# Stick-breaking attention summed by parts, with differences of v's rows

## The chip, the cores and the metric

The kernel runs on one core of one Trainium2 chip. The time is that of one execution on the device in microseconds (us), from the start to the end of the program on that core. The time given for a kernel is the median of several runs. The profile comes from one more execution, taken by the hardware profiler. PE is TensorE (PEld its weight loads), DVE is VectorE, ACT is ScalarE, POOL is GpSimd, and SP is the engine whose queue issues most of the DMAs.

## The reference, cut to what matters

The program is a trunk of two layers over 1024 tokens of 1024 channels; each layer is followed by a mixture of experts. The change touches one part of layer 0, stick-breaking attention with 8 heads of 64 channels:

```python
for blk in range(seq // Q_BLOCK):                      # Q_BLOCK = 128
    z = jnp.einsum('bhqd,bhkd->bhqk', qb, kb) * scale  # keys up to the block's end
    causal = kpos < qpos
    log_1m = jnp.where(causal, jax.nn.log_sigmoid(-z), 0.0)
    between = lax.cumsum(log_1m, axis=3, reverse=True) - log_1m
    wts = jnp.where(causal, jnp.exp(jax.nn.log_sigmoid(z) + between), 0.0)
    outs.append(jnp.einsum('bhqk,bhkd->bhqd', wts, vb))
```

So the weight of key k for a query is sigmoid(z_k) times the product of sigmoid(-z_j) over all later keys j. Everything is float32.

With pr_k the product of sigmoid(-z_j) from key k to the last key of the block, and pr = 1 behind the last key, the weight of key k is pr_(k+1) - pr_k, since sigmoid(z) = 1 - sigmoid(-z). A sum of (pr_(k+1) - pr_k) v_k over k equals v of the last key of the block plus the sum of pr_k (v_(k-1) - v_k), where v before the first key is 0.

## The kernel before

**Layer 0 ahead of attention.** The input projection gives the convolution's gate and value, q, k and v. Products are made in three matmuls of split operands (`mm3`, L260 to L264: high times high, high times low, low times high). The depthwise convolution of 31 taps runs on DVE (L482, 31 instructions of 1024 columns for each of 4 channel tiles) beside PE's projections. v is projected last (`vproj`, L528): for each of 8 tiles of 128 tokens, 24 matmuls whose stationary operand is the normalized input `hh`, `hl` and whose moving operand is v's weights give a PSUM tile `pvt` of 128 tokens by 512 channels; ACT copies it to `vsb` (L537). The calls of `vproj` stand between the steps of other work: three tiles behind the sums of squares of q and k (`qks`, L548, copied by DVE in L550), one each ahead of the stages of the convolution's layer norm (L576 to L596, sums over channels by matmuls on PE, L348), and two behind the last Silu (L600). Here the order of the instructions on each engine is set by a scheduler when the program is built, from priorities and its own costs; on the chip each engine takes its queue in order.

**The attention loop.** From L614 on, the order on ACT, DVE, PE and POOL is the order of the program. There are 4 pairs of heads (c), 8 query tiles each (t), taken in the order 3, 2, 1, 0, 4, 5, 6, 7; a tile's keys are taken from the last in blocks of up to 512 (bi counts them), so that there are 48 steps. A step works on 128 queries of two heads and n keys, n being 128 to 512. In loop turn s the program issues:

- `scores(s+1)`: matmuls of q and k to `z` (L653), and on the diagonal block the mask (L657);
- `mod_close`: two transposes on PE (`pmc`, L289) and a reduce on DVE (L290), which end a piece of an unrelated product, the layers' modulation vectors;
- `breaks(s)`: on ACT the sigmoid of -z (s1, L669) and of z (s2, L671) for both heads; on DVE the edge column of `pr` (1 at the start, L673, or the carry, L675), the running product of s1 from the last key to the first (two scans, L678), and the weights `w` = s2 times pr one column on (L681);
- `turn(s-1)`: n/128 transposes for each head to PSUM (`pt`, L690) and ACT's copy of them to `wt` (L692);
- `values(s-2)`: matmuls of `vsb` and `wt` to `po` (L703); at the end of a group of four query tiles ACT copies `po` to `o` (L708);
- `mod_open`, in most turns: 16 matmuls of the next modulation piece (`pm`, L277), DVE's copy of the sums to `modev` (L280), and the issue on SP of the loads of a later piece;
- in 24 turns, a part of the next pair's q or k: copies on ACT (L631, L632) and a subtraction on POOL (L634).

`pm` and `pmc` share one PSUM buffer, `pt` and `po` have one each, and `z` has four.

**After it** comes the output projection (from L774), whose order is again that of the program; its weights are loaded during the loop. It begins with ACT's and DVE's split of the weights (L252, L253).

## Time and profile before

| | |
|---|---|
| median of 3 runs | 2169.33 us (2169.12 to 2172.84) |
| the profiled execution | 2171.37 us, span 2169.6 us |
| busy over the span | PE 1863.1 us (86%), DVE 1429.3 (66%), ACT 989.7 (46%), POOL 424.9 (20%) |
| v's projection and the layer norm | about 229 to 318 us of the span |
| attention loop, first scores to last values | about 326 to 554 us |
| mean granted TensorE clock, in parts of the full one | 0.935 |

A page of the profile gives busy times of each engine and its instructions by line. Busy time of PE is modelled at its end, since matmuls overlap. A line such as `L280 DVE COPY modev<-pm 128x256 f32 x39 | 16.4, 420 | 10.2 <-PE pm L277 10.1` means: 39 instructions, 16.4 us busy, 420 ns each; the engine stood idle for 10.2 us just ahead of them, and PE's instruction of line 277 ended 10.1 us of that. In a timeline a line begins with start and length in us.

### The profile page before, as it was taken

What the parts mean: (1) busy time and instruction counts of PE and PEld (TensorE: products, weight loads), DVE (VectorE), ACT (ScalarE), POOL (GpSimd) and SP (SyncE); (2) the same over time, 40 slices, a digit from 0 to 9 for tenths busy, and PEclk for the clock granted to TensorE, in tenths of its full rate; (3) what the DMA queues carried; (4) which work ended last, traced back from release to release, by engine and by line L of the source; (5) the groups of instructions that cost most, each with busy time, mean ns of one, the idle gap of its engine ahead of it and who ended that gap; (6) DMA issues with size and microseconds to landing.
All of it is one profiled execution on the core that took longest, in us unless ns stands there. A gap on an engine that the chain in (4) does not pass through costs nothing. (4 is left out here: it accounts for less than half of the span.)

```text
span 2169.6 us, 27608 instructions
## 1 busy us (share of the span) xinstructions
PE 1863.1 (86%) x9580; PEld 1435.8 (66%) x9580; DVE 1429.3 (66%) x2110; ACT 989.7 (46%) x1388; POOL 424.9 (20%) x264
## 2 busy tenths in 40 slices
PE   6999987888886899988797599999868989888884
PEld 3788565555775677767676478887747777666663
DVE  4699657887588755676655266566784553677781
ACT  3212236776422544454544257784124342465660
POOL 1312004330233101110111132212331110211110
PEclk9999998999997899999999799999879999999997
DMA  8111004566522876897967521105325763899991
GB/s 304 58 39 59 20 20 137 194 208 220 176 107 92 279 232 208 238 321 226 291 190 245 148 92 44 44 20 186 117 103 183 201 198 114 259 299 296 309 308 28
DMA packets 104514, 369.52 MB, mean 170 GB/s; under 512 B 13680, under 2 KB 15024, under 8 KB 104240
## 3 DMA queue, kind: packets, MB, share of 16 engines
q1 hardware_dynamic: 91216, 319.29, 42.8%
q0 software_dynamic: 12928, 46.67, 9.6%
q8 instruction: 157, 2.57, 0.5%
q14 instruction: 117, 0.96, 0.1%
q10 hardware_dynamic: 96, 0.03, 0.0%
HBM read 324.76 MB, written 41.19 MB: 169 GB/s over the span
## 5 line engine op out<-in xcount | busy, mean ns | idle before, releaser
L253 DVE TENSOR_TENSOR wt<-raw,wt 128x1024 fp32r<-128x1024 f32 x384 | 459.1, 1222 | 144.7 <-ACT wt L252 116.2
L252 ACT ACTIVATE wt<-raw 128x1024 fp32r<-128x1024 f32 x384 | 395.5, 1059 | 213.0 <-DMA raw<-in_ex_w_dram 165.8
L262 PE MATMUL h<-wt,xtF 128*128 128x512 f32 x512 | 217.2, 424 | 15.1 <-PEq L1423 5.2
L263 PE MATMUL h<-wt,xtF 128*128 128x512 f32 x512 | 209.1, 408 | 6.7 <-issue 6.7
L264 PE MATMUL h<-wt,xtF 128*128 128x512 f32 x512 | 209.4, 409 | 4.3 <-issue 3.7
L482 DVE SCALAR_TENSOR_TENSOR cacc<-u,vecs,cacc 128x1024 f32<-128x1024 f32 x116 | 149.5, 1289 | 3.5
L262 PE MATMUL yp<-wt,xtF 128*128 128x512 f32 x256 | 109.5, 428 | 29.4 <-ACT xtF L1231 25.2
L253 POOL TENSOR_TENSOR wl<-raw,wh 128x1024 fp32r<-128x1024 f32 x32 | 84.4, 2658 | 243.8 <-ACT wh L252 243.8
L262 PEld LDWEIGHTS h<-wt,xtF 128*128 128x128 f32 x512 | 101.4, 198 | 44.1 <-issue 18.2
L264 PEld LDWEIGHTS h<-wt,xtF 128*128 128x128 f32 x512 | 101.0, 197 | 31.9 <-issue 5.9
L263 PEld LDWEIGHTS h<-wt,xtF 128*128 128x128 f32 x512 | 101.8, 199 | 29.0 <-issue 9.0
L262 PE MATMUL pout<-wouth,ch 128*128 128x512 f32 x256 | 110.3, 431 | 3.3 <-ACT ch L252 1.7
L264 PE MATMUL yp<-wt,xtF 128*128 128x512 f32 x256 | 107.6, 420 | 6.4 <-DVE xtF L1232 6.2
L1212 ACT ACTIVATE xtF<-pxt 128x512 fp32r<-128x512 f32 x64 | 34.9, 594 | 162.0 <-PE pxt L1211 146.6
L263 PE MATMUL pout<-woutl,ch 128*128 128x512 f32 x256 | 103.9, 406 | 2.8 <-DVE woutl L253 2.8
L263 PE MATMUL yp<-wt,xtF 128*128 128x512 f32 x256 | 106.2, 415 | 0.0
L264 PE MATMUL pout<-wouth,cl 128*128 128x512 f32 x256 | 104.1, 407 | 0.1
L262 PEld LDWEIGHTS yp<-wt,xtF 128*128 128x128 f32 x256 | 51.8, 203 | 50.3 <-ACT xtF L1231 30.9
L277 PE MATMUL pm<-raw,condb 128*32 128x256 f32 x768 | 63.1, 451 | 19.0 <-DMA raw<-in_mod_w_dram 13.5
L1200 POOL DMA_INDIRECT out_dram<-y,sidx x16 | 30.7, 1918 | 237.0 <-DVE y L1240 196.0
L1213 DVE TENSOR_TENSOR xtF<-pxt,xtF 128x512 fp32r<-128x512 f32 x64 | 41.2, 685 | 53.4 <-ACT xtF L1212 53.3
L1500 POOL DMA_INDIRECT xg<-h2d,idx x45 | 53.6, 1190 | 83.6 <-PE h L262 30.8
(400 smaller groups left out, 4304.0 us busy)
## 6 DMA issues: line engine op xcount, KB each, us to landing
raw<-in_ex_w_dram SPq DMA_DIRECT2D x384, 512.0 KB, 6.0
raw<-in_mod_w_dram SPq DMA_DIRECT2D x96, 512.0 KB, 4.6
raw<-in_ev_w_dram SPq DMA_DIRECT2D x16, 512.0 KB, 4.4
raw<-in_od_in_dram SPq DMA_DIRECT2D x16, 512.0 KB, 4.3
h2d<-x SPq DMA_DIRECT2D x14, 512.0 KB, 2.6
xs<-in_x_dram SPq DMA_DIRECT2D x8, 512.0 KB, 7.8
raw<-in_ev_out_dram SPq DMA_DIRECT2D x8, 512.0 KB, 4.9
x<-in_x_dram SPq DMA_DIRECT2D x8, 512.0 KB, 4.4
```

Source lines behind the costliest of these rows:

```text
L252: nc.scalar.activation(hi, raw, AF.Copy)
L253: (lo_eng or nc.vector).tensor_tensor(lo, raw, hi.bitcast(F32), op=ALU.subtract)
L262: nc.tensor.matmul(out, ah, bh, start=start, stop=False)
L263: nc.tensor.matmul(out, ah, bl, start=False, stop=False)
L264: nc.tensor.matmul(out, al, bh, start=False, stop=stop)
L277: nc.tensor.matmul(pm[32 * g:32 * g + 32, 0:256], self.condb[:, k, :], raw[k // 4][:, g, :], start=k < 4, stop=k >= 4)
L482: nc.vector.scalar_tensor_tensor(y if j < CW - 1 else acc[:, c, :], u[:, j:j + S], self.vec("ev_dw_w", 4 * j + c), y, op0=ALU.mult, op1=AL ...
L1200: nc.gpsimd.indirect_dma_start(out=xacc, out_offset=bass.IndirectOffsetOnAxis(ap=col, axis=0), in_=y[0:n], in_offset=None, compute_op=ALU.add)
L1212: nc.scalar.activation(xt[:, q, 0], px, AF.Copy)
L1213: nc.vector.tensor_tensor(xt[:, q, 1], px, xt[:, q, 0].bitcast(F32), op=ALU.subtract)
L1500: self.nc.gpsimd.indirect_dma_start(out=dst, out_offset=None, in_=self.h2d[l], in_offset=bass.IndirectOffsetOnAxis(ap=col, axis=0))
```

## The change

v is now projected with channels on partitions: for each of 4 channel tiles and both halves of the tokens, 24 matmuls with the weights as the stationary operand give 128 channels by 512 tokens. ACT copies the column of the last token of each of the four 128-token tiles to `vlast` and the whole tile to one half of a buffer `vdiff` (it takes the place of one of the convolution's two input buffers). DVE subtracts each token's column from the one before it. One unit later PE turns the result into rows by four transposes, and ACT copies these into `vsb`. In the attention loop `pr` itself is turned and multiplied with `vsb`; the sigmoid of z, the edge column and the product w go, and `pr` has three buffers. When a group of four query tiles is done, ACT writes `o` in four pieces of 128 columns, each with the matching column of `vlast` added.

```diff
-        def vproj(ts):
-            pv = [psA.tile([P, HS], F32, name="pvt", tag="big") for _ in ts]
...
-            for t in ts:
-                nc.scalar.activation(vsb[:, t, :], pv[t - ts[0]], AF.Copy)
+        diffs, both = {}, up.tile([P, CW - 1 + S], F32, name="vdiff", tag="u")
+        def vproj(us):
+            for u in us:
+                c, hf = divmod(u, 2)
+                pv = psA.tile([P, HS], F32, name="pvt", tag="big")
+                sl, n = slice(HS * hf, HS * hf + HS), slice(P * c, P * c + P)
+                for q, (wh, wl) in enumerate(vw):
                     for k in range(4):
-                        self.mm3(pv[t - ts[0]], hh[:, 4 * q + k, sl], hl[:, 4 * q + k, sl], wh[:, k, :], wl[:, k, :],
+                        self.mm3(pv, wh[:, k, n], wl[:, k, n], hh[:, 4 * q + k, sl], hl[:, 4 * q + k, sl],
                                  q == 0 and k == 0, q == 1 and k == 3)
+                d = diffs[u] = both[:, HS * (u % 2):HS * (u % 2) + HS]
+                nc.scalar.activation(vlast[:, c, 4 * hf:4 * hf + 4], pv[:, P - 1::P], AF.Copy)
+                nc.scalar.activation(d, pv, AF.Copy)
+                nc.vector.tensor_tensor(d[:, 1:HS], pv[:, 0:HS - 1], d[:, 1:HS], op=ALU.subtract)
+                if hf:
+                    nc.vector.tensor_tensor(d[:, 0:1], vlast[:, c, 3:4], d[:, 0:1], op=ALU.subtract)
+                else:
+                    nc.vector.tensor_scalar(d[:, 0:1], d[:, 0:1], -1.0, None, op0=ALU.mult)
+                if u:
+                    vrows(u - 1)
+        def vrows(u):
+            c, hf = divmod(u, 2)
+            d, pt = diffs.pop(u), psA.tile([P, 4, P], F32, name="pvr", tag="big")
+            for j in range(4):
+                nc.tensor.transpose(pt[:, j, :], d[:, P * j:P * j + P], self.ident)
+            nc.scalar.activation(vsb[:, 4 * hf:4 * hf + 4, P * c:P * c + P], pt, AF.Copy)
...
         vproj((6, 7))
+        vrows(7)
         p1.close()
...
-            pr = w3.tile([P, 2, HS + 1], F32, name="pr", tag="pr")
-            w = ws_[s] = w3.tile([P, 2, HS], F32, name="w", tag="w")
+            pr = ws_[s] = w3.tile([P, 2, HS], F32, name="pr", tag="pr", bufs=3)
...
-            for hd in range(2):
-                nc.scalar.activation(s2[:, hd, 0:n], z[hd][:, 0:n], AF.Sigmoid, scale=rq[:, t, c, 0, hd:hd + 1])
-            if bi == 0:
-                nc.vector.memset(pr[:, :, n:n + 1], 1.0)
-            else:
-                nc.vector.tensor_copy(pr[:, :, n:n + 1], carry[0][:, :, 0:1])
...
-            nc.vector.tensor_tensor(w[:, :, 0:n], s2[:, :, 0:n], pr[:, :, 1:n + 1], op=ALU.mult)
...
-                nc.scalar.activation(o[:, c, sl], po[0], AF.Copy)
+                for j in range(4):
+                    u = t // 4 * 4 + j
+                    nc.scalar.activation(o[:, c, P * u:P * u + P], po[0][:, P * j:P * j + P], AF.Identity,
+                                         bias=vlast[:, c, u:u + 1])
```

## Rows read from the trace of the kernel before

**Rows 1.** The first line of the page.

```profile
span 2169.6 us, 27608 instructions
```

**Rows 2.** Busy time of each engine (count of instructions) in three stretches, with the granted TensorE clock, the DMA engines' busy share and GB/s.

```profile
229.00:318.00 89.00, 88.82 (x468) 54.30 (x466) 52.60 (x86) 24.69 (x38) 4.71 (x2) 1.00 0.04 12
318.00:326.00 8.00, 2.49 (x30) 1.22 (x34) 4.33 (x6) 7.56 (x13) 2.52 (x2) 0.77 0.44 131
326.00:554.00 228.00, 188.57 (x1810) 127.69 (x1804) 178.39 (x280) 160.16 (x291) 70.14 (x44) 0.92 0.56 188
```

The columns are PE, PEld, DVE, ACT and POOL, after the stretch and its length.

**Rows 3.** PE's groups by line from 326 to 554 us: busy time, mean ns, and the idle time of PE ahead of them with what ended it.

```profile
L653 PE MATMUL z<-ks,qs 128*128 128x512 f32 (+3 forms) x192 | 53.5, 403 | 1.8 <-ACT s L671 0.9 <-POOL ks L634 0.5 <-DVE ks L634 0.4
...
L690 PE MATMUL pt<-ident,w 128*128 128x128 f32 x288 | 43.7, 293 | 11.8 <-DVE pr L673 7.9 <-DVE pr L675 2.2 <-DVE w L681 1.7
...
L289 PE MATMUL pmc<-ident,modev 128*128 128x128 f32 x78 | 17.4, 307 | 23.1 <-DVE modev L280 22.9
...
L304 PE MATMUL pmt<-ident,mcol 128*32 128x128 f32 x2 | 0.5, 269 | 2.6 <-DVE mcol L320 2.6
```

**Rows 4.** The timeline of one full step (512 keys), PE and DVE.

```profile
386.08 0.44 PE L289 MATMUL pmc<-ident,modev 128*128 128x128 f32 x2 [1.32 <-DVE modev L280]
...
386.56 0.17 DVE L290 TENSOR_REDUCE mcol<-pmc 128x2 f32<-128x8 f32 x1 [0.53 <-PE pmc L289]
...
386.71 2.45 DVE L678 TENSOR_TENSOR_SCAN pr<-s,pr 128x512 f32<-128x512 f32 x2
...
389.26 1.23 DVE L681 TENSOR_TENSOR w<-s,pr 128x1024 f32<-128x1024 f32 x1
...
390.40 0.42 DVE L280 COPY modev<-pm 128x256 f32<-128x256 f32 x1
...
390.88 0.44 PE L289 MATMUL pmc<-ident,modev 128*128 128x128 f32 x2 [0.44 <-DVE modev L280]
```

**Rows 5.** PE's timeline around a short step (256 keys and fewer).

```profile
456.60 0.43 PE L289 MATMUL pmc<-ident,modev 128*128 128x128 f32 x2
...
460.27 0.43 PE L289 MATMUL pmc<-ident,modev 128*128 128x128 f32 x2
```

**Rows 6.** Groups by line from 326 to 554 us on DVE, ACT and POOL.

```profile
L681 DVE TENSOR_TENSOR w<-s,pr 128x1024 f32<-128x1024 f32 (+3 forms) x48 | 51.9, 1081 | 5.2
L671 ACT ACTIVATE s<-z,rqk 128x512 f32<-128x512 f32 (+3 forms) x96 | 50.6, 588 | 0.0
...
L634 POOL TENSOR_TENSOR ks<-qk,ks 64x512 fp32r<-64x512 f32 x28 | 48.0, 1714 | 40.6 <-ACT ks L632 36.8 <-issue 2.8
...
L692 ACT ACTIVATE wt<-pt 128x1024 f32<-128x1024 f32 (+3 forms) x48 | 39.1, 814 | 53.9 <-PE pt L690 53.7
...
L634 POOL TENSOR_TENSOR qs<-qk,qs 64x512 fp32r<-64x512 f32 x14 | 19.2, 1370 | 61.6 <-ACT qs L632 61.4
...
L708 ACT ACTIVATE o<-po 128x512 f32<-128x512 f32 x7 | 4.2, 602 | 0.2 <-PE po L703 0.2
```

**Rows 7.** PE's timeline in the loop: of the six waits ahead of pt the first and the last, and of the ten waits of over 1.14 us ahead of pmc the first and the last.

```profile
337.79 1.97 PE L690 MATMUL pt<-ident,w 128*128 128x128 f32 x8 [4.67 <-DVE pr L673]
...
360.14 0.69 PE L289 MATMUL pmc<-ident,modev 128*128 128x128 f32 x2 [2.12 <-DVE modev L280]
...
523.35 0.44 PE L289 MATMUL pmc<-ident,modev 128*128 128x128 f32 x2 [1.65 <-DVE modev L280]
...
551.41 1.06 PE L690 MATMUL pt<-ident,w 128*128 128x128 f32 x8 [1.70 <-DVE w L681]
```

**Rows 8.** ACT's groups by line and shape from 326 to 554 us: a sigmoid of 128 columns from PSUM.

```profile
L669 ACT ACTIVATE s<-z,nrq 128x128 f32<-128x128 f32 x16 | 4.9, 357 | 0.0
```

**Rows 9.** PE's timeline in the output projection: four transposes between matmuls of 512 columns.

```profile
571.89 0.60 PE L847 MATMUL pto<-ident,x 128*128 128x128 f32 x4
...
572.56 0.40 PE L263 MATMUL pout<-woutl,ch 128*128 128x512 f32 x1
```

**Rows 10.** Groups by line from 229 to 318 us.

```profile
L585 DVE TENSOR_TENSOR acc<-acc,rb_ps 128x512 f32<-128x512 f32 x8 | 4.9, 683 | 0.8 <-PE rb_ps L360 0.8
...
L537 ACT ACTIVATE vsb<-pvt 128x512 f32<-128x512 f32 x7 | 4.1, 593 | 22.5 <-PE pvt L264 22.5
...
L550 DVE COPY qkssev<-qks 128x512 f32<-128x512 f32 x2 | 1.4, 692 | 15.7 <-PE qks L548 15.7
```

**Rows 11.** Timelines of DVE (first line, the convolution's last tap) and PE (the others) in that stretch and at its end.

```profile
274.78 1.27 DVE L482 SCALAR_TENSOR_TENSOR acc<-u,vecs,cacc 128x1024 f32<-128x1024 f32 x1
...
287.57 1.06 PE L348 MATMUL ss<-acc,ones 128*32 128x512 f32 x8
...
317.25 0.39 PE L263 MATMUL pvt<-wl,hh 128*128 128x512 f32 x1
317.48 0.40 PE L264 MATMUL pvt<-wh,hl 128*128 128x512 f32 x1
319.42 1.07 PE L277 MATMUL pm<-raw,condb 128*32 128x256 f32 x16 [1.54 <-issue]
```

**Rows 12.** The timeline of POOL and DVE around one of POOL's pairs of products.

```profile
378.95 4.33 POOL L634 TENSOR_TENSOR ks<-qk,ks 64x512 fp32r<-64x512 f32 x2 [4.58 <-ACT ks L632]
...
380.94 1.26 DVE L678 TENSOR_TENSOR_SCAN pr<-s 128x512 f32<-128x512 f32 x1
...
382.12 2.24 DVE L678 TENSOR_TENSOR_SCAN pr<-s 128x512 f32<-128x512 f32 x1
```

## The prediction

> **What bounds the kernel now.** The head of the page comes first [rows 1]: the profiled execution has a span of 2169.6 us and took 2171.37, so 1.8 lie around the span; the median of the runs shown, 2169.33, is 2.0 below that execution. The table by stretches is next [rows 2]. Two stretches matter. From 229 to 318 us, where v is projected, PE is busy 88.82 of 89 us: there whatever PE does in addition is paid. From 326 to 554 us is the attention loop, 228 us for 48 steps, and no engine fills it: PE 188.6, DVE 178.4, ACT 160.2. So in that stage something goes in a circle. PE's groups by line, with the idle time ahead of each and what ended it, name it [rows 3]: of the 39.4 us that PE stands idle (228 less 188.6), 23.1 come ahead of the two transposes called pmc, which close a piece of the modulation product and need DVE's copy modev, and 11.8 ahead of pt, the turn of the weights w, which need DVE's product; 2.6 and 1.8 come ahead of pmt and z. The timeline of one full step shows the circle [rows 4]: pmc on PE at 386.08, DVE's small reduce at 386.56, two scans until 389.16, the product w at 389.26, the copy modev at 390.40, and the next pmc at 390.88, after PE stood idle for 0.44. The round is 4.80 us, and all of it is DVE in its queue order plus the hop to PE and back. PE's own work in it is 4.80 - 0.44 = 4.36 us. In a short step [rows 5] pmc follows pmc after 3.67 us with no idle time noted on PE: there PE already sets the pace.

> **The change part by part.** In the attention loop three things go: 96 second sigmoids, 50.6 us of ACT; 48 products w, 51.9 us of DVE [rows 6]; and DVE's small fill of the edge column in each step. ACT's share is worth nothing by itself: ACT waits for PE's pt in the stage, and the sigmoids that remain are ahead of the scans in its queue. DVE's share lies on the circle. From the start of w to the start of the copy behind it are 1.14 us [rows 4], so DVE's round falls from 4.80 to 3.66 and PE's 4.36 is late next: a full step gains its idle 0.44 and no more. The stage therefore cannot give more than PE's 39.4 us, and I work out what stays. Of the waits ahead of pmc, those below 1.14 go altogether; the ten above it, the first and last of which are in [rows 7] and which sum to 16.6, keep 16.6 - 10 x 1.14 = 5.2. The waits ahead of pt are six, 4.67 the first and 1.70 the last [rows 7], with 1.79, 1.78, 1.45 and 0.42 between; each loses the product's 1.23 [rows 4] and together they keep 5.2. The 2.6 ahead of pmt stays, since its chain is not touched. Of the 1.8 ahead of z half waits for the second sigmoid and goes, 0.9 stays. That leaves 13.9 and gives 39.4 - 13.9 = 25.5 us. Bounds: nothing at the one end, the full 39.4 at the other; I take 25.5 because the rounds are told one by one. [...]

> The output of each group of four query tiles is now written by four ACT instructions of 128 columns with a bias, not one of 512: 8 x 4 = 32 of them. The nearest row is a sigmoid of 128 columns, 0.357 [rows 8], against 0.60 for the one that goes [rows 6]: 8 x (4 x 0.357 - 0.60) = 6.6 us more on ACT. Behind them in ACT's queue stand the next step's sigmoids, for which the scans wait; ACT has just lost 50.6 us, so I put 1.5 of the 6.6 on the path (0 to 6.6).

> In the projection the 192 matmuls stay, with the roles of weights and moving operand exchanged: no cost. Added are 32 transposes, four per unit. Four of the same kind stand between such matmuls later in the kernel [rows 9]: from their start to the second matmul behind them are 0.67 us, of which one matmul is 0.23, the distance of dense ones [rows 11]. So 0.44 a unit and 8 x 0.44 = 3.5 us, all paid since PE has no idle time there (0 to 5). DVE gets a subtraction of 512 columns, nearest row 0.68 [rows 10], and an operation on one column, nearest the small reduce's 0.17 [rows 4]: 0.85 a unit. About five of the eight fall beside the convolution, which ends at 276.05 while PE asks for its result at 287.57 [rows 11]; those I cost at nothing. If that cover is gone they cost up to 5 x 0.85 = 4.3. Two fall in the chain of the layer norm: 1.7. Behind the last matmul PE stood idle for 1.54 until the norm's last product [rows 11]; now a small ACT copy, a copy of 0.59 [rows 10], 0.68, 0.17 and 0.44 of transposes stand there, about 2.1 with the small copy at a third of the large one, so 0.6 is new, and 0.3 more as an estimate of the hops between engines. ACT's eight additional evictions of 0.59 are hidden (ACT is busy 24.7 of 89 us [rows 2]), except some at the end, ahead of the first copies of q and k: 1.0. The loss before the loop is 3.5 + 1.7 + 0.9 + 1.0 = 7.1.

> Sum on the profiled execution: -25.5 - 2 + 1.5 + 7.1 = -18.9, from 2171.4 to 2152.5; on the median 2150.4. I say **2150**. What follows the loop starts with weights that landed before and shifts as a whole.

> **Rivals.** (B) The loop gives all of PE's idle time. For it: a round that starts earlier lets the next one start earlier, and DVE's total after the cut, 178.4 - 51.9 = 126.5 us, is far below PE's. Against: the first waits of the loop are start-up, and the rounds with a long wait are those beside GpSimd. -39.4 - 3 + 1.5 + 7.1 = -33.8: 2136.

> (C) The blocked rounds keep their length. A scan takes 1.26 alone and 2.24 when it starts beside a running GpSimd product [rows 12]; and each of GpSimd's 42 products in the stage [rows 6] can hold one DVE instruction. Until now the product w took a part of these hits; without it the scans take them, and the ten long waits do not shrink: 11.4 less gained, and no clock. -25.5 + 11.4 + 1.5 + 7.1 = -5.5: 2164. [...]

> (D) Slower: DVE's queue jams before the loop. DVE takes its instructions in order, and in the projection stretch it stood 15.7 us in two waits for the sums qks, with the convolution queued behind [rows 10]. If the subtractions of the first three units are queued as early and each holds DVE for as long as those (7.85), 23.6 us are added ahead of the layer norm and so of the loop: -18.9 + 23.6 = +4.7, 2174. It decides from 18.9 us of such waits on. For it: the place in the queue is set without knowledge of real times. Against: the two existing waits already hold DVE while the first unit is computed, and PE fills a delayed norm with the units that are left.

> (E) The circle does not close tighter, as the scans wait for the sigmoids behind ACT's pieces of output, evictions and copies of q and k: if two thirds of the 25.5 us go that way, 8.5 are left, and the 8.6 added eat them: 2169. Against it: after the cut ACT's work in the stage is 160.2 - 50.6 + 6.6 = 116 us of 228, and it stands idle for 53.9 us ahead of the evictions of pt alone [rows 6].

> **How the numbers follow.** Forecast 0.50 (own range 2143 to 2158), B 0.17, C 0.17, D 0.11, E 0.05. A measurement of this kernel tells 0.2% (4.3 us) from no change. Faster than 2165: the forecast, B and three quarters of C, 0.80. Same, 2165 to 2173.7: the rest of C and E, 0.09. Slower: D, 0.11. For 8 in 10 the range reaches 2134 to 2167: past B's value by the bounds of its terms, and to the upper side of C.

> **What would show it.** Right: in the loop PE's waits ahead of pmc fall from 23.1 to some 5 us, the stage from 228 to about 202, PE is busy over 0.9 of it, and the loop starts some 7 us later. The step of the transposes is wrong if the projection grows by more than 5 us; the step of the cover if DVE's convolution ends more than 5 us later. The whole is wrong if a full round keeps 4.8 us with PE waiting for the copy, or if DVE waits for pvt for longer than 15 us in total.

## The result and the profile after

The changed kernel takes 2119.32 us (median of 4 runs, 2112.63 to 2124.39), the kernel before 2169.22 beside it (4 runs): a ratio of 0.9755, 95% interval 0.9711 to 0.9799. The prediction had the sign; the gain is 50 us where 19 were forecast, and the time lies below the range. The profiled execution took 2124.39 us, 47.0 less than the one before [rows 1].

The head of the page, which answers to [rows 1], with the line of busy times:

```profile
span 2122.6 us, 27537 instructions
...
PE 1856.0 (87%) x9612; PEld 1436.1 (68%) x9612; DVE 1388.1 (65%) x2030; ACT 956.6 (45%) x1332; POOL 419.5 (20%) x264
```

By stretches, as in [rows 2] (PE, PEld, DVE, ACT and POOL, then granted clock, DMA share, GB/s): the attention loop from the first scores to the last value matmul, the projection, and MoE 0 from its first token index to its last scatter.

```profile
330.70:519.90 189.20, 176.61 (x1812) 123.07 (x1808) 133.45 (x184) 119.62 (x217) 63.53 (x44) 0.95 0.67 226
229.00:321.30 92.30, 92.00 (x496) 57.23 (x495) 57.70 (x101) 30.32 (x54) 4.72 (x2) 1.00 0.04 12
668.70:1184.70 516.00, 452.79 (x2006) 358.40 (x2005) 325.13 (x393) 246.99 (x315) 72.59 (x48) 0.94 0.78 244
```

Cut the 47 us along these marks (first scores 330.7 for 326.9, loop 189.2 for 227.9, and so on): the start +3.8, the loop -38.7, from the loop to the first token index +2.1, MoE 0 -12.8, all behind it -1.5. So there are three things to explain: the loop gave 38.7 and not 26; the start cost 3.8 and not 7.1; and MoE 0, of which not an instruction was changed, gave 12.8.

PE's groups in the loop, which answer to [rows 3] (count, busy time, mean ns, and idle time ahead with what ended it):

```profile
L675 PE MATMUL z<-ks,qs 128*128 128x512 f32 (+3 forms) x192 | 51.3, 390 | 0.8 <-POOL ks L656 0.5 <-DVE ks L656 0.4
L704 PE MATMUL pt<-ident,pr 128*128 128x128 f32 x288 | 42.3, 281 | 5.3 <-DVE pr L693 4.7 <-ACT wt L706 0.5
...
L289 PE MATMUL pmc<-ident,modev 128*128 128x128 f32 x78 | 16.2, 290 | 3.0 <-DVE modev L280 3.0
...
L304 PE MATMUL pmt<-ident,mcol 128*32 128x128 f32 x2 | 0.5, 270 | 3.3 <-DVE mcol L320 3.3
```

The wait ahead of pmc has fallen from 23.1 to 3.0, that ahead of pt from 11.8 to 5.3. And the same instructions take less time: z 51.3 for 53.5, pt 42.3 for 43.7, pmc 16.2 for 17.4. Together PE is busy 176.6 us for 188.4 with the same 1812 instructions, at a granted clock of 0.95 for 0.92. The step of [rows 4], in which 4.80 us lay from pmc to pmc with 0.44 of waiting, now has PE without a wait and takes 4.20:

```profile
376.68 0.44 PE L289 MATMUL pmc<-ident,modev 128*128 128x128 f32 x2
376.95 1.04 PE L704 MATMUL pt<-ident,pr 128*128 128x128 f32 x8
377.92 1.09 PE L717 MATMUL po<-wt,vsb 128*64 128x128 f32 x16
378.95 1.07 PE L277 MATMUL pm<-raw,condb 128*32 128x256 f32 x16
379.95 0.96 PE L675 MATMUL z<-ks,qs 128*128 128x384 f32 x4
380.75 0.28 PE L679 MATMUL z<-maskb,identb 128*128 128x128 bf16 x2
380.88 0.39 PE L289 MATMUL pmc<-ident,modev 128*128 128x128 f32 x2
```

### The profile page after: what moved, and what is told of

Same layout as the page of the kernel before. It is cut to its first block, busy times and chain, and to the rows that moved or that the text cites. A ratio compares the mean times of both kernels' runs of the same rounds, so it can differ in the third digit from the quotient of the medians.

```text
span 2122.6 us, 27537 instructions
## 1 busy us (share of the span) xinstructions
PE 1856.0 (87%) x9612; PEld 1436.1 (68%) x9612; DVE 1388.1 (65%) x2030; ACT 956.6 (45%) x1332; POOL 419.5 (20%) x264
## 3 DMA queue, kind: packets, MB, share of 16 engines
q8 instruction: 157, 2.57, 0.5%
## 5 line engine op out<-in xcount | busy, mean ns | idle before, releaser
L262 PE MATMUL h<-wt,xtF 128*128 128x512 f32 x512 | 213.6, 417 | 13.4 <-issue 5.7
L263 PE MATMUL h<-wt,xtF 128*128 128x512 f32 x512 | 205.6, 402 | 6.9 <-issue 6.9
L264 PE MATMUL h<-wt,xtF 128*128 128x512 f32 x512 | 206.4, 403 | 1.1 <-DVE xtF L1229 1.0
L262 PE MATMUL yp<-wt,xtF 128*128 128x512 f32 x256 | 113.7, 444 | 35.2 <-ACT xtF L1247 30.4
L262 PEld LDWEIGHTS h<-wt,xtF 128*128 128x128 f32 x512 | 99.7, 195 | 34.7 <-issue 12.8
L264 PEld LDWEIGHTS h<-wt,xtF 128*128 128x128 f32 x512 | 98.8, 193 | 29.3 <-issue 3.7
L264 PE MATMUL yp<-wt,xtF 128*128 128x512 f32 x256 | 111.6, 436 | 8.0 <-DVE xtF L1248 4.1
L263 PEld LDWEIGHTS h<-wt,xtF 128*128 128x128 f32 x512 | 99.7, 195 | 27.6 <-issue 8.1
L263 PE MATMUL yp<-wt,xtF 128*128 128x512 f32 x256 | 109.6, 428 | 0.0
L264 PE MATMUL pout<-wouth,cl 128*128 128x512 f32 x256 | 103.9, 406 | 0.1
L262 PEld LDWEIGHTS yp<-wt,xtF 128*128 128x128 f32 x256 | 54.5, 213 | 57.9 <-ACT xtF L1247 36.0
L264 PEld LDWEIGHTS yp<-wt,xtF 128*128 128x128 f32 x256 | 53.3, 208 | 25.8 <-DVE xtF L1248 11.7
```

The source lines that it names most:

```text
L262: nc.tensor.matmul(out, ah, bh, start=start, stop=False)
L263: nc.tensor.matmul(out, ah, bl, start=False, stop=False)
L264: nc.tensor.matmul(out, al, bh, start=False, stop=stop)
```

## The experiments

All times of this table are read from the profile of each kernel in the same way, in us: when the first scores begin, the loop to the end of the last value matmul, PE's busy and idle time and the granted clock in it, MoE 0 from the first token index to the last scatter, and PE's waits in MoE 0 that end with nothing that the profile shows ("issue").

| kernel | first scores | loop | PE busy | PE idle | clock | MoE 0 | issue waits | span |
|---|---|---|---|---|---|---|---|---|
| before | 326.9 | 227.9 | 188.4 | 39.4 | 0.92 | 528.7 | 23.1 | 2169.6 |
| before_again | 327.8 | 225.6 | 186.9 | 38.8 | 0.93 | 525.9 | 21.9 | 2171.1 |
| turns_late | 327.5 | 225.5 | 186.2 | 39.3 | 0.93 | 526.6 | 27.1 | 2169.7 |
| turns_128 | 336.0 | 223.9 | 184.2 | 39.6 | 0.95 | 532.3 | 22.6 | 2182.1 |
| before_turns | 326.6 | 227.9 | 188.6 | 39.3 | 0.92 | 507.9 | 11.2 | 2143.4 |
| rows_old_loop | 329.8 | 229.3 | 189.7 | 39.6 | 0.91 | 515.6 | 16.5 | 2163.8 |
| product_back | 330.3 | 226.7 | 190.0 | 36.7 | 0.90 | 515.5 | 18.0 | 2157.8 |
| sigmoid_back | 330.9 | 195.9 | 177.6 | 18.3 | 0.96 | 514.3 | 17.7 | 2124.3 |
| the change | 330.7 | 189.2 | 176.7 | 12.5 | 0.95 | 515.9 | 15.4 | 2122.6 |
| after_again | 330.3 | 188.7 | 175.8 | 12.9 | 0.96 | 514.8 | 17.2 | 2117.1 |
| after_third | 330.7 | 188.2 | 175.8 | 12.4 | 0.97 | 516.3 | 18.9 | 2119.7 |
| after_turns96 | 329.1 | 188.8 | 175.9 | 12.9 | 0.96 | 526.4 | 25.7 | 2139.3 |
| low_on_vector | 329.4 | 184.1 | 173.3 | 10.8 | 0.98 | 508.9 | 12.0 | 2105.5 |
| low_again | 330.1 | 185.5 | 174.9 | 10.5 | 0.96 | 511.0 | 13.7 | 2102.9 |
| rows_late_low | 329.8 | 183.3 | 172.8 | 10.5 | 0.98 | 521.9 | 24.0 | 2113.3 |

### The loop: the product or the sigmoid

The changed kernel with one of the two removed things put back, as dead work:

```diff
+            w = w3.tile([P, 2, HS], F32, name="w", tag="w")
+            nc.vector.tensor_tensor(w[:, :, 0:n], s1[:, :, 0:n], pr[:, :, 0:n], op=ALU.mult)
```

> The changed kernel, with one VectorE product of s1 and the running products added in every step behind the scans; nothing reads it, so the output stays the reference's. If VectorE's round of scans and product set the loop's pace (my theory: the old loop's idle time and its lower clock both hang on it), the loop from the first scores to the last value matmul goes from 190 us back to 215 to 228 us, TensorE's busy time in it for the same instructions from 177 back to 184 to 189 us with a granted clock of 0.92 to 0.93, and the whole is 25 to 38 us over the changed kernel. If ScalarE's second sigmoid was what had set the pace, the loop stays within 5 us of 190 us at a clock of 0.95, and the whole within 5 us of the changed kernel. If the faster clock comes from elsewhere than the loop's gaps, idle time comes back and TensorE's busy time stays at 177 us. MoE 0 should keep the changed kernel's 514 us if its gain is one of code that was taken out, and be anything from 514 to 527 us if it is chance.

Measured: 2156.78 us, 0.9923 of before (0.9886 to 0.9959), 41 us over the changed kernel in the same rounds (2115.65) and a little past the 38 that I had set as the most. Its loop, and there PE's groups z, pt, pmc and DVE's product:

```profile
330.27:557.00 226.73, 190.03 (x1812) 130.37 (x1808) 177.97 (x232) 119.34 (x216) 71.17 (x44) 0.90 0.57 189
```

```profile
L675 PE MATMUL z<-ks,qs 128*128 128x512 f32 (+3 forms) x192 | 52.2, 397 | 0.4 <-DVE ks L656 0.4
L706 PE MATMUL pt<-ident,pr 128*128 128x128 f32 x288 | 46.1, 298 | 8.0 <-DVE pr L693 5.7 <-ACT ch L252 2.1 <-ACT wt L708 0.2
...
L289 PE MATMUL pmc<-ident,modev 128*128 128x128 f32 x78 | 18.2, 318 | 26.2 <-DVE modev L280 26.2
...
L697 DVE TENSOR_TENSOR w<-s,pr 128x1024 f32<-128x1024 f32 (+3 forms) x48 | 56.0, 1167 | 1.7
```

Nobody reads this product, and yet the old loop is back: 26.2 us of waits ahead of pmc, PE idle for 36.7 us, a clock of 0.90, and PE busy 190.0. So DVE's round sets the pace, and the 12 us of PE's busy time go and come with PE's idle time, not with the new rows of v or the shorter ACT.

```diff
+            s2 = w3.tile([P, 2, HS], F32, name="s2", tag="s2")
+            for hd in range(2):
+                nc.scalar.activation(s2[:, hd, 0:n], z[hd][:, 0:n], AF.Sigmoid, scale=rq[:, t, c, 0, hd:hd + 1])
```

> The changed kernel, with the second sigmoid of every step put back on ScalarE behind the first; nothing reads it, so the output stays the reference's. If VectorE's round set the old loop's pace, ScalarE has room for these 56 activations and the loop stays at 190 to 195 us, and the whole within 6 us of the changed kernel. If ScalarE's queue was what the old loop waited for, the loop goes to 205 us or more and the whole by 15 us or more.

Measured: 2125.45 us, 9.8 over the changed kernel in the same rounds, where the theory of DVE's round allowed 6; a loop of 195.9, just past the 195 that it allowed and far from the rival's 205.

```profile
L675 PE MATMUL z<-ks,qs 128*128 128x512 f32 (+3 forms) x192 | 51.2, 386 | 5.2 <-ACT s L693 2.4 <-POOL ks L656 2.3 <-DVE ks L656 0.4
...
L289 PE MATMUL pmc<-ident,modev 128*128 128x128 f32 x78 | 15.9, 285 | 6.9 <-DVE modev L280 6.7
```

So ACT's 50 us were not quite worthless: with DVE's product gone, the second sigmoid would be the next thing in the way, for some 7 us (z waits 2.4 us for it, and pmc 6.9 for 3.0). PE's busy time stays at 177.6: the waits it adds are few (PE idle 18.3 us for 12.5) and the clock holds (0.96 for 0.95).

One more term of the loop, the four pieces of output:

```diff
-                for j in range(4):
-                    u = t // 4 * 4 + j
-                    nc.scalar.activation(o[:, c, P * u:P * u + P], po[0][:, P * j:P * j + P], AF.Identity,
-                                         bias=vlast[:, c, u:u + 1])
+                sl = slice(HS * (t // 4), HS * (t // 4) + HS)
+                nc.scalar.activation(o[:, c, sl], po[0], AF.Copy)
```

> The changed kernel with the attention output copied in one piece a group and not four, without the bias that holds v's last row, so this row is missing from the output. The prediction put 1.5 us on the path for the three additional instructions a group (0 to 6.6). If that holds the loop falls from 189 to 187.5 us; if ScalarE hides them, it stays at 189 us within 0.7 us; if all of it is on the path it falls to 183 us.

Measured: a loop of 188.3, as in the three profiles of the changed kernel (188.2 to 189.2). The pieces cost nothing that can be seen. Only the loop is read here: the output is another, so the tokens go to other experts (1929 matmuls of PE in MoE 0 for 2005), and what follows can't be compared.

### The start

The old loop behind the new projection, whose VectorE instructions subtract nothing here, so that plain rows come out:

```diff
-                nc.vector.tensor_tensor(d[:, 1:HS], pv[:, 0:HS - 1], d[:, 1:HS], op=ALU.subtract)
+                nc.vector.tensor_tensor(d[:, 1:HS], pv[:, 1:HS], self.zero.to_broadcast([P, HS - 1]), op=ALU.subtract)
...
```

> The loop of the kernel before (two sigmoids, scan with carry column, product, one output copy), with the changed kernel's projection: channels on partitions, the same VectorE, ScalarE and TensorE instructions before the loop, but the VectorE ones leave v's values as they are, so that plain rows come out. By the prediction's terms the first scores come at 326.9 + 6.2 = 333 us and the whole is 6 us over the kernel before. By the trace of the changed kernel it is the transposes alone, first scores at 330.7 us and the whole some 4 us over the kernel before. If the new layout of v's rows had a part in the loop's gain, the loop is shorter than 228 us by 3 us or more.

Measured: first scores at 329.8, loop 229.3, so the new rows have no part in the loop's gain. But the whole is 2153.33 us, 0.9911 of before (0.9883 to 0.994): 18 us faster, where both accounts had it 4 to 6 slower. In the profiled execution, the slowest of its runs, the start and the loop are 4 us longer and MoE 0 is 13 us shorter than in the kernel before. This run, a miss of mine, is what showed that MoE 0's gain has nothing to do with the loop.

The changed kernel with the transposes left out, and v's differences copied unturned:

```diff
-            d, pt = diffs.pop(u), psA.tile([P, 4, P], F32, name="pvr", tag="big")
-            for j in range(4):
-                nc.tensor.transpose(pt[:, j, :], d[:, P * j:P * j + P], self.ident)
-            nc.scalar.activation(vsb[:, 4 * hf:4 * hf + 4, P * c:P * c + P], pt, AF.Copy)
+            d = diffs.pop(u)
+            nc.scalar.activation(vsb[:, 4 * hf:4 * hf + 4, P * c:P * c + P], d.rearrange("p (j n) -> p j n", j=4),
+                                 AF.Copy)
```

> The changed kernel without the 32 transposes: the differences go into v's tile unturned, by one ScalarE copy a unit as before, so the output is another. If the transposes are all that the new projection costs TensorE, the first scores come 3 to 4 us earlier than the changed kernel's 330.5 us, at 326.5 to 327.5 us, with the VectorE and ScalarE instructions of the new projection still there. If those too stand on the path (the prediction's 3.6 us), only the transposes' own time on the path goes and the first scores stay at 328 us or later.

Measured: the last matmul of v ends at 316.2 instead of 321.3, but the first scores stay at 330.5. ACT's timelines tell why, of the changed kernel first and then of this one (start, length, what it did):

```profile
318.18 1.33 ACT L621 ACTIVATE acc<-acc,vecs 128x512 f32<-128x512 f32 x2
...
321.40 0.59 ACT L544 ACTIVATE vdiff<-pvt 128x512 f32<-128x512 f32 x1
...
323.60 0.60 ACT L558 ACTIVATE vsb<-pvr 128x512 f32<-128x512 f32 x1 [1.11 <-PE pvr L557]
324.09 0.62 ACT L654 ACTIVATE qs<-qk 64x512 fp32r<-64x512 f32 x1
```

```profile
320.55 2.70 ACT L620 ACTIVATE acc<-acc,vecs 128x512 f32<-128x512 f32 x4 [1.38 <-DVE acc L616]
323.25 0.63 ACT L556 ACTIVATE vsb<-vdiff 128x512 f32<-128x512 f32 x1
323.96 0.63 ACT L653 ACTIVATE qs<-qk 64x512 fp32r<-64x512 f32 x1
```

The loop begins with ACT's first copy of q, which stands in ACT's queue behind v's last copy and behind the layer norm's last silu (`acc<-acc`). In the changed kernel v's last copy is late (323.60), while its silus have ended at 319.51. Without the transposes the silus are late: the last four begin at 320.55 and end at 323.25. So this run does not give the transposes' price. With them gone the scheduler built another order, in which the layer norm's last products on PE (`rb_ps`) begin at 318.09 and not at 314.48.

Other traces tell more. ACT's first copy of q begins at 324.09 for 320.32 in the kernel before, 3.8 later. In the kernel before the last matmul of v ends at 317.88 and the silus at 320.42, so there are some 2.4 us of room behind it. In the changed kernel it ends at 321.30, 3.4 later, and v's last copies and turn take 2.8 more. In before_turns (next section), 32 transposes stand in the old projection: its last matmul ends at 319.88, within that room, and ACT's first copy of q (320.42) and the first scores (326.6) come as without them. So the transposes are paid only as far as they and the steps behind the last matmul go past the silus.

A version that moves the last unit's turn and copy behind ACT's copies of q and k, with v's last differences kept in v's own tile (and the edit of the next section but one):

```diff
...
+        ptl, vl = psZ.tile([P, 4, P], F32, name="pvl", tag="z"), vsb[:, 4:8, P * 3:P * 3 + P]
+        for j in range(4):
+            nc.tensor.transpose(ptl[:, j, :], vl[:, j, :], self.ident)
+        nc.scalar.activation(vl, ptl, AF.Copy)
         scores(0)
...
```

> The changed kernel with two edits: the low parts of q and k in the loop on VectorE (the version before), and the last unit of v's differences kept in v's own tile, turned and copied only after ScalarE's six copies of q and k. If the loop's start hangs on ScalarE's queue, where those copies stand behind the last unit's copy (324.1 us in the changed kernel, 320.3 in the kernel before), the first scores come 3 to 4 us earlier than in the version before, at 325.5 to 327 us, and the whole is 3 to 4 us under it, near 2108 us. If something else sets the start (the layer norm's chain, as where the transposes were left out), they stay at 329 us or later.

Measured: 2115.05 us and first scores at 329.8, a miss. ACT's first copy of q does come 1.6 us earlier, at 322.48, but no more, since ACT still waits for PE's last unit, whose last matmul ends at 321.42 behind the other 28 transposes; and half of the 1.6 is given back, as the four transposes now stand ahead of the scores on PE, and take 1.12 us there, where four at 321.26 take 0.60:

```profile
329.06 1.12 PE L767 MATMUL pvl<-ident,vsb 128*128 128x128 f32 x4
329.82 1.24 PE L683 MATMUL z<-ks,qs 128*128 128x512 f32 x3
```

### MoE 0: where the instructions lie

Both kernels once more, unaltered:

> The kernel before unaltered, profiled once more. If the length of its MoE 0 belongs to the program (where its TensorE instructions lie in memory, and so where TensorE waits for the next block of them), the stretch from the first token index to the next layer's (914.6 us in its first profile; 901 to 904 us in the five profiles of programs with the new projection) is 912 us or more, and TensorE stands for about 5 us ahead of the transposes of a hidden block in the last experts of MoE 0. If it was chance, it is 901 to 905 us. The loop should be 228 us within 1 us.

> The changed kernel unaltered, profiled once more. If the 12.7 us that went inside MoE 0 (from the first token index to the last scatter, 527.1 to 514.4 us) belong to the program, it is 514 us again within 2 us. If they were chance of one execution, MoE 0 differs from 514 us by 5 us or more. The loop should be 190 us and the first scores at 330.7 us, both within 1 us.

Measured: MoE 0 is 525.9 us in the kernel before and 514.8 in the changed one, beside 528.7 and 515.9 in their first profiles, and the stretch to the next layer's index is 911.5, just under the 912 expected, and 901.2. The old loop takes 225.6 us this time, so its length varies by more than the 1 us that I had allowed. (The lengths of MoE 0 here and in the table reach to the end of the last scatter; the expectation's 527.1 and 514.4 reach to its start, 1.5 less.) It is no chance of one execution. In the kernel before, the stop among the transposes of a hidden block is there in both profiles. This is its first timeline on PE, then the same place in the changed kernel:

```profile
1184.69 0.39 PE L264 MATMUL h<-wt,xtF 128*128 128x512 f32 x1
1185.75 0.52 PE L1229 MATMUL pht<-ident,slF 128*128 128x128 f32 x3 [0.67 <-PEq L1387]
1191.54 0.37 PE L1229 MATMUL pht<-ident,slF 128*128 128x128 f32 x1 [5.26 <-issue]
```

```profile
1146.48 0.39 PE L264 MATMUL h<-wt,xtF 128*128 128x512 f32 x1
1147.62 0.63 PE L1245 MATMUL pht<-ident,slF 128*128 128x128 f32 x4 [0.75 <-PEq L1403]
1148.01 0.47 PE L262 MATMUL h<-wt,xtF 128*128 128x512 f32 x1
```

PE stands still for 5.26 us in the middle of four transposes that read one tile and write one tile, and the profile finds nothing that the fourth waits for. In the view of the DMA queues, the 9 us around it hold one packet of another kind (queue, kind, packets, MB, share of 16 engines):

```profile
q1 hardware_dynamic: 613, 2.22, 73.5%
q8 instruction: 1, 0.02, 0.6%
```

The page has 157 packets of this queue with 2.57 MB in all, 16 KB each: instructions are brought while the kernel runs, by DMA engines that are busy with weights for three quarters of MoE 0 (the DMA share of 0.78 above). The trace has the time of each packet. The one above moves from 1189.21 to 1190.12, and PE goes on at 1191.54, 1.42 later. In all 15 profiles of the table PE's "issue" waits of over 0.4 us in MoE 0 number 108, and every one ends 1.20 to 1.77 us behind the end of a packet of this queue. Of PE's 611 other waits of that length there 44 do, which is what chance gives with a packet every 9.5 us. The profile does not say for which engine a packet is; that PE stands still for its own instructions is what I read from so regular a distance.

The theory of the difference: PE stops where a new block of its instructions (one packet) begins and the block is late. Where that is in the work depends on how many instructions PE has had ahead of it, and the changed kernel has 32 transposes more. Why a block is late isn't shown: the packets that PE waits for take as long as the others (0.95 us for 0.98, medians), so they begin late and are not slow. The traces do not give the number of PE's instructions in a packet. By the theory 32 more transposes move the stops, and a number that fills whole packets puts them back; that 128 would be such a number was not shown ahead of the run. If more transposes help by themselves, 128 shorten MoE 0 as 32 do.

The kernel before with 32 idle transposes in the projection, then with the same 32 in the second layer, then with 128 in the projection:

```diff
+                pt = psA.tile([P, 4, P], F32, name="pvr", tag="big")
+                for j in range(4):
+                    nc.tensor.transpose(pt[:, j, :], self.ident, self.ident)
```

> The kernel before, with 32 transposes of a constant among the matmuls of the old projection, four behind each unit, into PSUM that nobody reads; all else as before and the output the reference's. It gives TensorE's instructions the same count as in the changed kernel. If the gain inside MoE 0 hangs on where TensorE's blocks of instructions end, the stretch from the first token index to the next layer's falls to 901 to 905 us and the whole to 8 to 15 us under the kernel before, although 3.5 us of transposes are added. If it hangs on the new projection in another way (tiles elsewhere in SBUF, ScalarE's and VectorE's instructions), the stretch stays at 912 us or more and the whole is 2 to 5 us over the kernel before.

> The kernel before, with the same 32 idle transposes, but behind MoE 0, in the second layer's norm, so that TensorE's instructions up to the end of MoE 0 lie where they lay before. If the gain of the version with transposes in the projection came from where TensorE's instructions lie, the stretch from the first token index to the last scatter of MoE 0 keeps its 524 to 527 us, with some 20 us or more of TensorE's waits for nothing that the profile shows (issue) up to the next layer's index, and only what lies behind can change. If idle transposes help in another way, or the pairs of runs drift, the whole falls by 15 us or more here too.

> [...]

Measured: with 32 transposes that do nothing, the kernel before falls to 2151.12 us, 0.9905 (0.988 to 0.993), 21.6 us faster and more than I expected (8 to 15); MoE 0 has 507.9 us. Behind MoE 0 they change nothing: 0.9991 (0.9969 to 1.0012), MoE 0 526.6. With 128 the old length is back, 532.3 us (to the next index 919.6; one run), and so is the stop, one instruction further on:

```profile
1194.03 0.63 PE L1233 MATMUL pht<-ident,slF 128*128 128x128 f32 x4 [0.66 <-PEq L1391]
1198.72 0.58 PE L262 MATMUL h<-wt,xtF 128*128 128x512 f32 x1 [4.06 <-issue]
```

What was left open was whether this holds for the change itself. The changed kernel with 96 idle transposes at its very start, where PE waits for its first data, so that PE has 128 more than the kernel before:

```diff
+        for _ in range(24):
+            pt = psA.tile([P, 4, P], F32, name="idle", tag="big")
+            for j in range(4):
+                nc.tensor.transpose(pt[:, j, :], self.ident, self.ident)
         mods(range(W0AT))
```

> [...] The loop should stay at 189 us within 2 us; the start is later by up to 20 us.

Measured: MoE 0 526.4 us with 25.7 us of issue waits, and the stop among these transposes is back, one instruction ahead of that of the kernel before:

```profile
1148.97 0.41 PE L1249 MATMUL pht<-ident,slF 128*128 128x128 f32 x2 [0.66 <-PEq L1407]
1153.65 0.69 PE L1249 MATMUL pht<-ident,slF 128*128 128x128 f32 x2 [4.27 <-issue]
```

The whole is 2142.01 us, 0.9862 of before (0.9829 to 0.9896), where the unaltered changed kernel has 2119.01 in the same rounds, 0.9749 (0.9724 to 0.9774). Its first scores come at 329.1, so the added transposes themselves cost nothing there. Counted in PE's matmuls from the first token index, all five profiles with the old number of instructions or 128 more stop at number 1158 to 1160, 1484 to 1487 and 1891 to 1893, for over 0.4 us, and none of the ten with 32 more does; six of those ten stop at 1762 or 1763 instead. Not every stop moves: at 837, 1253, 1749 and 1977 there are stops with either number of instructions, so these have another reason than the count. (The run no_turns has the old number too, but another output and so other work, 1937 matmuls in MoE 0 for 2005.) How long the stops are varies. The version rows_late_low, with 32 more as well, has 24.0 us of such waits (one of 7.2), which the count alone doesn't explain.

The waits are not all of it. Of the 12.8 us that the change gains in MoE 0, 7.7 are issue waits (15.4 for 23.1); PE is busy 3.4 us less there (452.8 for 456.2) and waits 1.6 less for other things. I take these for what follows from fewer stops, but no run shows it.

### GpSimd beside the scans

The low parts of q and k in the loop on VectorE instead of GpSimd:

```diff
-                    part(0, i, LATE.index(s), slice(HS, S), nc.gpsimd)
+                    part(0, i, LATE.index(s), slice(HS, S), nc.vector)
...
-                part(c + 1, q, hd, slice(HS * hf, HS * hf + HS), nc.gpsimd)
+                part(c + 1, q, hd, slice(HS * hf, HS * hf + HS), nc.vector)
```

> The changed kernel with the subtractions that make the low parts of q and k in the loop on VectorE and not on GpSimd. If the contention between GpSimd's products and VectorE's scans costs nothing in the changed loop, since TensorE sets its pace, the loop stays at 189 us or grows by what the 40 or so VectorE instructions of about 0.5 us each put into VectorE's queue (up to 10 us). If that contention is what holds the rest of TensorE's idle time (12.5 us), the loop falls by 3 us or more, to 186 us or less, and this version beats both.

> The version with the low parts of q and k on VectorE, unaltered. If its loop's 5 us reach the end, its median is 3 to 8 us under that of the changed kernel in the same rounds, and the loop is 184 us within 1 us. MoE 0 was 508.9 us in its first profile: 507 to 511 us if the length belongs to the program, and anything from 508 to 522 us if it is chance of one execution.

> The changed kernel unaltered, beside the version with the low parts on VectorE. Loop 189 us within 1 us, MoE 0 514 to 516 us as in its two profiles so far, the median at 2115 to 2120 us.

Measured: 2111.69 us, then in five rounds 2106.87 (2100.58 to 2110.91) beside the changed kernel's 2119.01 (2118.15 to 2123.38): this version beats both kernels, by 12 us where 3 to 8 were expected. The loop is 184.1 and 185.5 us, some 4 under the changed kernel's 188.2 to 189.2; half of that is idle time of PE (10.5 to 10.8 for 12.4 to 12.9), so the contention does not hold the rest of it. The other 8 of the 12 us lie in MoE 0 (511.0 for 516.3) and behind it, where code lies elsewhere too; I don't count those for the edit. DVE's groups in the loop, of the changed kernel and of this version:

```profile
L693 DVE TENSOR_TENSOR_SCAN pr<-s 128x512 f32<-128x512 f32 (+3 forms) x64 | 68.5, 1113 | 3.4 <-ACT s L690 3.4
L693 DVE TENSOR_TENSOR_SCAN pr<-s,pr 128x512 f32<-128x512 f32 x32 | 42.2, 1358 | 2.3 <-ACT s L690 2.3
```

```profile
L693 DVE TENSOR_TENSOR_SCAN pr<-s 128x512 f32<-128x512 f32 (+3 forms) x64 | 50.1, 824 | 1.8 <-ACT s L690 1.5
L693 DVE TENSOR_TENSOR_SCAN pr<-s,pr 128x512 f32<-128x512 f32 x32 | 40.3, 1301 | 1.0 <-ACT s L690 0.8
L656 DVE TENSOR_TENSOR ks<-qk,ks 64x512 fp32r<-64x512 f32 x30 | 20.5, 685 | 2.6 <-ACT ks L654 2.2
...
L656 DVE TENSOR_TENSOR qs<-qk,qs 64x512 fp32r<-64x512 f32 x14 | 9.6, 686 | 1.4 <-ACT qs L654 0.8
```

Beside GpSimd the same 96 scans take 110.7 us, alone 90.4: the contention costs DVE 20 us, 70% of the 28.7 us of subtractions that it takes over here (of the 30.1, two with 1.4 were its own before).

## Why the prediction was right and wrong

**The idle time of the loop: right.** From 39.4 to 13.9 was forecast, with pmc 5.2, pt 5.2, pmt 2.6 and z 0.9; measured are 12.5, with 3.0, 5.3, 3.3 and 0.8. DVE's round was the circle, PE's own work is late next, and product_back shows it by putting the round back. For pmc the mechanism held wait by wait: the first, 2.12 us, became 0.80, and of 22 waits five are left. That pt came out at 5.3 for 5.2 is luck: five waits of the old six were to stay, the first with 3.44, and there are nine, the longest 1.11, some of them new at the end of the loop.

**The granted clock: the term that was mis-sized.** No run shows the 2 us that the sum has for the clock (B's sum has 3, C's none); measured are 11.8 us less of busy time for the same matmuls (176.6 us for 188.4). In the traces of before and of the change the granted clock has two values, 0.50 and 1.00. So a clock of 0.92 over 227.9 us is 0.08 / 0.5 = 16% or 36 us at the lower one; the changed loop's 0.955 over 189.2 is 17 us. Eight transposes take 1.97 us at 337.79, where the granted clock is 0.50, and 1.06 at 551.41, where it is 1.00 [rows 7]. So the 19 us that are no longer spent at 0.50 give 9 to 10 of the 11.8, an estimate (a factor of 1.86 by these two times, of 2 by the two values); the rest is open. From 345 us on the granted clock of the loop before falls to 0.50 seven times, each time in or right behind a wait of PE of 1.45 to 2.23 us; that of the changed loop falls once, behind one of 2.51. Other waits of that length pass without a fall. The row to work from was there [rows 2]: 36 us at 0.50 are worth up to 18 by the same estimate, and a loop without its gaps was to get back more than a ninth of that.

**The output pieces and the start: too dear.** The 1.5 for the pieces is nothing (one_piece). Of the start's 7.1 only 3.8 came. The transposes do lengthen PE's projection by about what was set (3.0 of 3.5; from the first to the last matmul of v 89.3 us for 86.3), but "all paid" is not what the runs show: in before_turns the same 32 cost the start nothing. The 3.6 for copies, subtractions and the last turn were added on top, while in the trace the later of two chains counts, v's last turn or the layer norm's silus, not the sum. One row was misread there: the 1.54 of idle time [rows 11] stands ahead of the modulation product `pm`, not of a product of the norm, and lies on neither chain. The cover held: the convolution's last tap ends at 279.26 for 276.05, within the 5 us that I had set.

**"What follows the loop ... shifts as a whole": the step that failed.** It took the same instructions behind the loop to need the same time. They don't: with 32 more transposes on PE the places at which PE stops move (issue waits in MoE 0 15.4 us for 23.1), and MoE 0 gave 12.8 us, for which the sum had nothing. With the old places (after_turns96 beside after_third) 23.0 of the changed kernel's 55.7 us in those rounds are gone; in the two profiles, 19.6 us apart, 10 lie in MoE 0 and 9 behind it. Why 9 there, where the profiles of before and after differ by only 1.5, stays open. What is left, 32.7 us, agrees with the trace: the first token index comes 32.8 us earlier (668.7 for 701.6). So some 33 us are the change's own, where 18.9 were forecast. 2142.01 us lies inside the range that was given, but near its lower end: the clock's 9.8 us too few and the start's and the pieces' 4.8 too many are in it.

**The rivals.** B, all of PE's idle time: no, 12.5 us stay. C, blocked rounds keep their length: the contention is there, the price isn't. (Its scan of 1.26 us [rows 12] was not alone: it began beside the end of GpSimd's first product, and the second product, 2.10 us long, ran beside it.) The scans did take hits that the product had taken; those 96 scans took 63.7 + 40.2 = 103.9 us in the loop before, in these two groups of DVE's:

```profile
L678 DVE TENSOR_TENSOR_SCAN pr<-s 128x512 f32<-128x512 f32 (+3 forms) x64 | 63.7, 1035 | 2.3 <-ACT s L669 2.2
...
L678 DVE TENSOR_TENSOR_SCAN pr<-s,pr 128x512 f32<-128x512 f32 x32 | 40.2, 1298 | 2.3 <-ACT s L669 2.3
```

They now take 110.7. As DVE is busy for 133 of 189 us, PE hides most of it, and what is left is the 4 us that low_on_vector gains. The contention shows in the scan's mean time: the group of 64 takes 1113 ns each beside GpSimd's subtractions, and 824 in low_again, without them. D, a jam of DVE's queue: DVE waited 3.3 us for the copies of v, not the 18.9 from which it decides:

```profile
L545 DVE TENSOR_TENSOR vdiff<-pvt,vdiff 128x511 f32<-128x511 f32 x8 | 5.5, 684 | 3.3 <-ACT vdiff L544 3.3
```

E, ACT: no, but the second sigmoid alone, put back, costs 7 us, so it is the nearest thing to the bound.

## What to carry to other kernels

Where a stage has gaps and a granted clock under one, price the clock from its rows: part of the time at the lower level goes with the gaps, on top of the idle time (here 19 of 36 us). Steps of two chains that end at one queue are not added; take the later chain. And before a gain or a loss of some 10 us in untouched code is credited to an edit, put a block of idle instructions on that engine and see whether it moves.
